# Modulation weights of a two-layer diffusion backbone loaded as 1 MB transfers instead of groups of four

## The chip, the cores and the metric

The kernel runs on one core of one Trainium2 chip. The metric is the device time of one execution in microseconds; several executions are made and their median is given. One further execution is taken with the hardware profiler, and all rows below come from it. Everything is computed in float32 accuracy.

## The reference, cut to what matters

Two layers of a diffusion backbone work on 1024 latent tokens and 256 context tokens of width 1024. Each layer starts from modulation vectors: a conditioning vector, one for the latent tokens and one for the context, times a weight matrix `w_mod` of 1024 rows by 6144 columns, plus `b_mod`:

```python
sh1, sc1, gt1, sh2, sc2, gt2 = jnp.split(mod_lat, 6, axis=-1)
h = rms_norm(x, g1) * (1 + sc1) + sh1
aq, ak, av, bq, bk, bv, cq, ck, cv, co, cg, dq, dk, dv = split_proj(h @ w_in)
...
x = x + gt1 * mix_out([ya, yb, yc, yd], g_group, w_out)
h2 = rms_norm(x, g2) * (1 + sc2) + sh2
x = x + gt2 * conv_ffn(h2, w_up, conv_w, conv_b, w_down)
```

So the first third of the modulation vector (`sh1`, `sc1`) is wanted before the input projection of its layer can begin; the other two thirds are wanted only behind attention. Four attention-like mixers (A to D) read slices of the one projection.

## The kernel before, in words

`w_mod` of a layer is cut into three sections of 2048 columns. `mod_section` computes one section: with the two conditioning vectors as the stationary operand (`self.stat[:, k]`, 128 rows by 32 columns, two of them used), it streams the weights through TensorE, for eight blocks of 128 rows (`k`). The 2048 columns are four groups `g` of 512; the product of group `g` goes to partitions 32g to 32g+31 of one PSUM tile (`modps`), that is to one of four column groups of the array. The finished sums are copied to SBUF (`modrow`), turned to features on partitions by four small products (`modo`) and added to the bias.

There are six sections, 48 MB of weights in all. The first (layer 0, section 0) runs in `start`, ahead of everything, with 512 columns in a piece: four transfers of 256 KB and four products 128x512 for each `k`, from a pool of 12 buffers. The other five run inside `phase1` of the two layers, as filler: `run` asks the generator `mods` for a step at every fourth step of the dense projections, which themselves are mixed with group A's attention. There the pieces have 256 columns: four transfers of 128 KB and four products 128x256 for each of 16 steps, from a pool of four buffers. Each step's transfers are written one step ahead of their products.

The order on each engine isn't written by hand. The program is given to a scheduler, which gives every instruction a priority by its place in the code and, by its own estimate of times, puts on each engine what it thinks can start next. The resulting order is fixed at build time; each engine then works through its list strictly in order and waits on semaphores. All transfers are issued by SyncE (SP), also in order: a transfer that has to wait for its buffer or its data holds up all that stand behind it. All of them go through one hardware queue.

Names in the rows: `wmod` the modulation weights, `stat` the stationary operand, `modps`, `modrow`, `modo` as above; `pj` the products of the input projection, `whi`/`wlo` and `hh`/`hl` the two parts of its weights and inputs; `xi`/`xt` the token-major inputs and their transposes; `ssq`, `ss`, `rsbc` the sums of the norm; `kt`/`kT` the keys of group A and their transposes; `S`, `mT`, `O`, `Y` group A's scores, maxima, values and outputs; `sX`, `sA_qk` scratch in HBM. One product of two float32 operands leaves two MATMUL records in the trace; a projection product, whose operands are the narrower parts, leaves one.

Of the kernel before, what the change touches and what calls it, by code (L numbers as in the profile page):

```python
# [29 lines left out]
# column chunks of the input projection: (name, ((first column, width) of each piece))  # L30
# [12 lines left out]
NB = (12, 4, 4)  # L43
# the mixer's second products: the order of the buffers of its inputs and of its weights
# [3 lines left out]
class Net:  # L48
# [40 lines left out]
    def weight(self, pool, src, eng, bufs, tag, raws=2, w=512, rawp=None):  # L89
        """The two parts of a weight block [P, 512] loaded from src, its first w columns used."""  # L90
# [15 lines left out]
    def mm3(self, out, terms, first=True, last=True, **kw):  # L106
        """out += sum of lhs.T @ rhs over terms ((lh, ll), (rh, rl)), float32 accuracy."""
# [46 lines left out]
    def cond_vector(self, st):  # L154
        """stat[:, k, 0:2] = silu of c and of c_ctx, features on partitions; the rest is zero."""
# [26 lines left out]
    def vectors(self, l, tile, t):  # L182
        nc, a = self.nc, self.a
        vp = self.vecp
        r1 = tile(name="r1")[0:112, 0:P]
        r2 = tile(name="r2")[0:88, 0:P]
# [10 lines left out]
        # the gated half of the conv carries the 1/2 of silu(x) = x (1 + tanh(x/2)) / 2  # L197
# [5 lines left out]
    def mod_section(self, l, sec, pool, pp, tag, modT, w=256):  # L203
        """modT[:, 16 sec + i, v]: features 128 i of section sec (2048 columns); v 0 latent, 1 context.
        Yields the time of each of its pieces."""
        nc, a = self.nc, self.a
        acc = pp.tile([P, 512], F32, tag=tag, name="modps")

        def load(n):
            W = []  # L210
            for g in range(4):
                W.append(pool.tile([P, w], F32, tag="raw", name="wmod"))
                c0 = sec * 2048 + g * 512 + n // KD * w
                nc.sync.dma_start(W[g], a["w_mod"][l, n % KD * P:(n % KD + 1) * P, c0:c0 + w])
# [12 lines left out]
        rows = [pool.tile([P, w], F32, tag="raw", name="modrow") for _ in range(512 // w)]  # L227
        for x, row in enumerate(rows):
            nc.scalar.copy(out=row, in_=acc[:, x * w:(x + 1) * w])
        yield 0.3  # L230
        o = pp.tile([P, 512], F32, tag=tag, name="modo")
        for b in range(4):
            nc.tensor.matmul(o[:, 8 * b:8 * b + 8], rows[b * P // w][:, b * P % w:b * P % w + P], self.sel8, start=True, stop=True)
# [7 lines left out]
    def rstd_rows(self, xs, n, p, pp, tag, most):  # L241
        """rs[:, i] = rstd of token 128 i + partition, for the n tokens of xs [P, KD, n]; most: the most tokens in p."""
# [23 lines left out]
    def rstd_cols(self, xs, n, p, pp, tag, most=256):  # L266
        """The rstd of the n tokens of xs [P, KD, n], on every partition."""
# [10 lines left out]
    def modulated(self, xs, bc, hi, lo, scale, bias, p=None):  # L278
        """hi + lo = xs * bc * scale + bias, in xs or by way of tiles of p; scale, bias [P, KD]."""
# [38 lines left out]
    def load_x(self, i, p, pp, tag):  # L318
        """Tile i of xT from the token-major inputs."""
# [15 lines left out]
    def phase1(self, l, modT, dst):  # L335
        """Norm 1, input projection, group A's attention, the preparation of groups C and D (its pools in dst)."""
        nc = self.nc
        with ExitStack() as st:
# [17 lines left out]
            mp = self.sb(st, f"wmods{l}", bufs=4)  # L356
            mps = self.ps(st, f"wmodp{l}")

            def modulation():
                yield from self.mod_section(l, 1, mp, mps, "mod", modT)  # L360
                if l == 0:
                    self.vectors(1, lambda name: mp.tile([P, 256], F32, tag="raw", name=name), mps.tile([P, 512], F32, tag="mod", name="vt"))
# [45 lines left out]
    def start(self, modT, wp, pm, ep):  # L408
        """The first layer's inputs: xT, the vectors, the modulation of norm 1, the weights of group A's columns."""
        with ExitStack() as s2:  # L410
# [6 lines left out]
            for _ in self.mod_section(0, 0, mp, pm, "mm", modT, 512):  # L417
                pass
            self.vectors(0, lambda name: ep.tile([P, 512], F32, tag="st", name=name), pm.tile([P, 512], F32, tag="mm", name="vt"))
# [5 lines left out]
    def norm1(self, l, modT, W, nrm, np_, pm, ep):  # L425
        """Norm 1, and the projection of group A's columns."""
# [44 lines left out]
    def proj_tiles(self, chunk, W, tiles, pm, ep):  # L471
        """A chunk's columns for the tiles, token-major."""
# [14 lines left out]
    def proj_cols(self, W, blocks, queries, out, pm, ep):  # L487
        """Column blocks of a chunk for all tokens, feature-major; the first ones are queries."""
# [11 lines left out]
    def rope(self, i, src, ep):  # L500
        """Rotates the heads src [P, 6, 64] of latent tile i - 2."""
# [65 lines left out]
    def out_d(self, f, p, x, ep):  # L567
        """Group D's query (the tokens of each tile in reverse) or key heads 2 f, 2 f + 1."""
# [30 lines left out]
    # Rows 0..9 are the forward chunks in scan order, rows 32..41 the backward ones; time runs forward in each row.  # L599
    def mlstm_steps(self, l, st):  # L600
        """Yields the time of its pieces, or of other work to put between them, and None once the gates are done."""
# [16 lines left out]
        with ExitStack() as s2:  # L618
# [41 lines left out]
            # running maximum across the chunks: m <- max(m, amax) + cend  # L660
# [63 lines left out]
        # ---- chunk sweeps  # L724
# [8 lines left out]
        at = [list(range(NT)), [1, 0] + list(range(NT - 1, 1, -1))]  # the tiles in scan order  # L733
# [102 lines left out]
    def group_norm(self, y, i, grp, p):  # L836
        """Stores y / rms(y) times the gain, over the 256 columns of one head group of tile i."""
# [44 lines left out]
    def prep_q(self, qt):  # L882
        """QH[:, h], QL[:, h]: the two parts of query head h, each on both halves of the partitions."""
# [871 lines left out]
```

## Time and profile before

| | us |
|---|---|
| median of 3 runs | 3538.09 (3537.04 to 3539.44) |
| the profiled execution's span, first to last instruction | 3548.8 |
| PE busy | 3416.7 (96%) |
| DVE busy | 2173.3 (61%) |
| ACT busy | 1497.2 (42%) |
| POOL busy | 955.8 (27%) |
| DMA, mean | 106 GB/s |

The profiled execution is 10.7 us longer than the median run. A row of the timeline gives the start in us from the span's start, the length, the engine, the source line, the operation, out<-in, the shape and the number of records that were merged, and in brackets the idle time ahead of it. Matmuls are pipelined, so lengths of neighbours overlap: what one costs is read from the distance of starts. In a shape as 128*32 128x256, 128*32 is the stationary operand and 256 the columns streamed.

### The profile page before, as it was taken

Reading aid. Unit: us, or ns where it says so; the run is one execution under the profiler, and the core shown is the slowest. Engines: PE = TensorE matmul, PEld = TensorE weight load, DVE = VectorE, ACT = ScalarE, POOL = GpSimd, SP = SyncE. Lnnn points to the kernel's source line nnn. Section 1 sums busy time; section 2 is a strip of 40 time slices with the busy share of each in tenths; the row PEclk is TensorE's granted clock in tenths of the full one; section 3 lists DMA queues with packets and bytes.
Section 4 is the critical chain, followed back from the end, with each engine's and each line's share of the span. In section 5 each row is a group of like instructions: output and inputs, shape, how many; then the busy total and the mean of one; then the engine's idle time right before and its main releaser. Section 6 shows DMA issues by size and latency. Waiting matters only on the chain. (4 is left out here: it accounts for less than half of the span.)

```text
span 3548.8 us, 53999 instructions
## 1 busy us (share of the span) xinstructions
PE 3416.7 (96%) x19949; PEld 2719.4 (77%) x19949; DVE 2173.3 (61%) x4103; ACT 1497.2 (42%) x3010; POOL 955.8 (27%) x1069
## 2 busy tenths in 40 slices
PE   8999999999997999999999999999999879999998
PEld 4776678776885888888888676877778758888887
DVE  4455452775438777778454745554774388888745
ACT  5334332556544444444120534423565454445311
POOL 2423233231344222220000623324222343332000
PEclk9999999999998999999999999999999989999999
DMA  8534344415331222215222534236233322222621
GB/s 285 156 104 124 96 115 125 126 51 159 117 107 54 64 72 64 74 63 204 85 83 78 144 109 121 68 105 170 64 121 96 99 63 86 75 90 75 219 83 60
DMA packets 437679, 377.61 MB, mean 106 GB/s; under 512 B 123048, under 2 KB 381224, under 8 KB 437416
## 3 DMA queue, kind: packets, MB, share of 16 engines
q1 hardware_dynamic: 437416, 374.17, 34.2%
q8 instruction: 157, 2.57, 0.3%
q14 instruction: 106, 0.87, 0.1%
HBM read 279.69 MB, written 94.37 MB: 105 GB/s over the span
## 5 line engine op out<-in xcount | busy, mean ns | idle before, releaser
L112 PE MATMUL b<-g,w 128*128 128x512 f32 (+1 forms) x880 | 321.9, 368 | 0.0
L113 PE MATMUL b<-g,w 128*128 128x512 f32 (+1 forms) x880 | 320.8, 368 | 0.0
L111 PE MATMUL b<-g,w 128*128 128x512 f32 (+1 forms) x880 | 320.1, 368 | 0.0
L1652 DVE SCALAR_TENSOR_TENSOR xT<-b,modT,xT 128x512 f32<-128x512 f32 (+1 forms) x280 | 191.5, 695 | 201.0 <-PE b L113 200.5
L111 PE MATMUL pj<-whi,hh 128*128 128x512 f32 (+2 forms) x800 | 282.8, 355 | 12.9 <-ACT v L554 5.4
L112 PE MATMUL pj<-wlo,hh 128*128 128x512 f32 (+2 forms) x800 | 281.4, 352 | 3.0 <-DVE wlo L103 3.0
L113 PE MATMUL pj<-whi,hl 128*128 128x512 f32 (+2 forms) x800 | 280.8, 352 | 0.0
L1526 POOL TENSOR_TENSOR s<-raw 128x512 f32<-128x512 f32 x88 | 118.2, 1343 | 471.0 <-DVE w L1533 381.5
L111 PEld LDWEIGHTS pj<-whi,hh 128*128 128x128 f32 x800 | 152.8, 191 | 49.8 <-issue 11.6
L112 PEld LDWEIGHTS b<-g,w 128*128 128x128 f32 x880 | 165.6, 189 | 27.5
L111 PEld LDWEIGHTS b<-g,w 128*128 128x128 f32 x880 | 165.5, 189 | 27.5
L113 PEld LDWEIGHTS b<-g,w 128*128 128x128 f32 x880 | 165.3, 188 | 27.7
L112 PEld LDWEIGHTS pj<-wlo,hh 128*128 128x128 f32 x800 | 153.0, 191 | 36.9 <-issue 15.0
L113 PEld LDWEIGHTS pj<-whi,hl 128*128 128x128 f32 x800 | 152.4, 191 | 35.5 <-issue 17.0
L1555 DVE SCALAR_TENSOR_TENSOR cg<-u,vec,cg 128x512 f32<-128x512 f32 (+1 forms) x176 | 166.4, 989 | 10.1 <-ACT cg L1550 10.1
L1532 ACT CAST w<-s 128x512 fp32r<-128x512 f32 x176 | 107.0, 618 | 155.1 <-PE b L113 103.5
L86 ACT CAST w<-raw 128x512 fp32r<-128x512 f32 x88 | 54.0, 620 | 271.1 <-PE b L113 241.7
L112 PE MATMUL o<-yl,wohi 128*128 128x256 f32 x576 | 164.9, 287 | 0.9 <-DVE yl L87 0.9
L113 PE MATMUL o<-yh,wolo 128*128 128x256 f32 x576 | 165.5, 288 | 0.1
L111 PE MATMUL o<-yh,wohi 128*128 128x256 f32 x576 | 164.9, 289 | 0.7 <-ACT yh L86 0.7
L1533 DVE TENSOR_TENSOR w<-raw,w 128x512 fp32r<-128x512 f32 x154 | 131.4, 867 | 54.0 <-ACT w L1532 53.9
L103 POOL TENSOR_TENSOR wolo<-raw,wohi 128x512 fp32r<-128x512 f32 x80 | 103.8, 1298 | 162.3 <-ACT wohi L102 148.0
(364 smaller groups left out, 9852.4 us busy)
## 6 DMA issues: line engine op xcount, KB each, us to landing
raw<-in_w_up_dram SPq DMA_DIRECT2D x176, 256.0 KB
wmod<-in_w_mod_dram SPq DMA_DIRECT2D x320, 128.0 KB
raw<-in_w_down_dram SPq DMA_DIRECT2D x88, 256.0 KB
raw<-in_w_in_dram SPq DMA_DIRECT2D x80, 256.0 KB
raw<-in_w_out_dram SPq DMA_DIRECT2D x80, 256.0 KB
sG<-cv SPq DMA_DIRECT2D x22, 640.0 KB
graw<-sG SPq DMA_DIRECT2D x22, 640.0 KB
sG<-cv SPq DMA_DIRECT2D x22, 512.0 KB
```

The costliest lines, as they stand in the source:

```text
L86: nc.scalar.copy(out=hi, in_=src)
L103: eng.tensor_tensor(lo[:, 0:w], raw[:, 0:w], f32v(hi[:, 0:w]), ALU.subtract)
L111: nc.tensor.matmul(out, lh, rh, start=(first and i == 0), stop=False, **kw)
L112: nc.tensor.matmul(out, lh, rl, start=False, stop=False, **kw)
L113: nc.tensor.matmul(out, ll, rh, start=False, stop=(last and i == n - 1), **kw)
L1526: nc.gpsimd.tensor_tensor(s, x, y, op)
L1532: nc.scalar.copy(out=hi, in_=src)
L1533: nc.vector.tensor_tensor(out=lo, in0=src, in1=f32v(hi), op=ALU.subtract)
L1555: nc.vector.scalar_tensor_tensor(out=o[:, x0:x1], in0=u[:, x0 - d - c:x1 - d - c], scalar=self.cw[w][:, j:j + 1], in1=o[:, x0:x1], op0=ALU ...
L1652: nc.vector.scalar_tensor_tensor(out=xs, in0=o[:, 0:t1 - t0], scalar=modT[:, 40 + f, v:v + 1], in1=xs, op0=ALU.mult, op1=ALU.add)
```

## The change

A section is loaded in eight transfers of 128 rows by 2048 columns (1 MB, 8 KB in a row) in place of 32 of 256 KB or 64 of 128 KB. Each lands in one tile that holds the four groups side by side, and the four products, now always 512 columns wide, read it. In `start` the pool has three such buffers (12 of 512 columns before, the same bytes); in `phase1` it has one (8 KB per partition; four of 1 KB before). As a step is now a whole block of 128 rows in both places, a section takes 8 steps and 2 for its end, where it took 16 and 2 in `phase1`. The staging buffer of `load_kv` for group A now comes from the tag of the maxima (`M`) in place of a pool of its own, and `vectors` gets one tile in place of two. What else is in the difference is comments that were dropped, which only moves line numbers (L223 becomes L214).

```diff
-NB = (12, 4, 4)
...
+NB = (3, 4, 4)
...
-    def mod_section(self, l, sec, pool, pp, tag, modT, w=256):
...
+    def mod_section(self, l, sec, pool, pp, tag, modT):
...
-        def load(n):
-            W = []
+        for k in range(KD):
+            W = pool.tile([P, 4, 512], F32, tag="raw", name="wmod")
+            nc.sync.dma_start(W.rearrange("p g f -> p (g f)"), a["w_mod"][l, k * P:(k + 1) * P, sec * 2048:(sec + 1) * 2048])
+            yield 0.5
             for g in range(4):
-                W.append(pool.tile([P, w], F32, tag="raw", name="wmod"))
-                c0 = sec * 2048 + g * 512 + n // KD * w
-                nc.sync.dma_start(W[g], a["w_mod"][l, n % KD * P:(n % KD + 1) * P, c0:c0 + w])
-            return W
-
-        W = load(0)
-        steps = 512 // w * KD
-        for n in range(steps):
-            yield 0.5
-            k, o = n % KD, n // KD * w
-            for g in range(4):
-                nc.tensor.matmul(acc[32 * g:32 * g + 32, o:o + w], self.stat[:, k, :], W[g],
+                nc.tensor.matmul(acc[32 * g:32 * g + 32], self.stat[:, k, :], W[:, g],
                                  start=(k == 0), stop=(k == KD - 1), skip_group_check=True)
-            if n < steps - 1:
-                W = load(n + 1)
...
-            mp = self.sb(st, f"wmods{l}", bufs=4)
+            mp = self.sb(st, f"wmods{l}")
...
-            for _ in self.mod_section(0, 0, mp, pm, "mm", modT, 512):
+            for _ in self.mod_section(0, 0, mp, pm, "mm", modT):
...
-                for _ in self.load_kv(KV, lambda: lp.tile([P, 512], F32, tag="kt", name="kt", bufs=2),
...
+            for _ in self.load_kv(KV, lambda: self.ap_.tile([P, 512], F32, tag="M", name="kt", bufs=2),
```

With other pieces the scheduler makes another order. Three places of it follow, the kernel before first.

TensorE in layer 0's phase 1, third section (`modps`), among projection products (`pj`), before:

```order
1653 L223 MATMUL modps<-wmod,stat 32x256
1654 L113 MATMUL pj<-hh_485,wlo 128x256
1655 L111 MATMUL pj<-hh_485,whi 128x256
1656 L223 MATMUL modps<-wmod,stat 32x256
1657 L112 MATMUL pj<-hl_486,whi 128x256
1658 L113 MATMUL pj<-hh_485,wlo 128x256
1659 L111 MATMUL pj<-hh_485,whi 128x256
1660 L223 MATMUL modps<-wmod,stat 32x256
1661 L112 MATMUL pj<-hl_486,whi 128x256
```

and now, in the same stage:

```order
1312 L1116 MATMUL S<-QL,ks 128x256
1313 L1115 MATMUL S<-QH,ks 128x256
1314 L1116 MATMUL S<-QL,ks 128x256
1315 L214 MATMUL modps<-wmod,stat 32x512 x4
1316 L111 MATMUL pj<-whi,hh_442 128x272
1317 L112 MATMUL pj<-wlo,hh_442 128x272
1318 L113 MATMUL pj<-whi,hl_443 128x272
```

Products that stood alone between others, each behind its own transfer, now stand as a run of four behind one transfer. Counted over the five sections of phase 1, the 320 products stood in 198 runs (136 of one product, 23 of two, 18 of three, 21 of four); the 160 products now stand in 51.

SyncE at the program's start, around the end of the first section's loads (`wmod`), before:

```order
16 L214 DMA wmod<-in_w_mod_dram 128x512 x4
17 L96 DMA raw<-in_w_in_dram 128x512 x2
18 L214 DMA wmod<-in_w_mod_dram 128x512 x4
19 L96 DMA raw<-in_w_in_dram 128x512 x2
20 L322 DMA xi<-in_x_dram 128x1024 x4
21 L452 DMA cos<-in_cos_dram 128x512
```

and now, with the last two loads of that section in row 31 (three stand in row 8, ahead of all others of this kind):

```order
22 L434 DMA sX<-xT 1024x1x256
23 L211 DMA wmod<-in_w_mod_dram 128x2048
24 L96 DMA raw<-in_w_in_dram 128x512 x4
25 L211 DMA wmod<-in_w_mod_dram 128x2048
26 L96 DMA raw<-in_w_in_dram 128x512 x4
27 L310 DMA xi<-in_x_dram 128x1024 x2
28 L434 DMA sX<-xT 1024x1x256
29 L310 DMA xi<-in_x_dram 128x1024 x2
30 L434 DMA sX<-xT 1024x1x256
31 L211 DMA wmod<-in_w_mod_dram 128x2048 x2
```

The section's last loads have moved behind all inputs `xi`, eight blocks of projection weights and three stores of `sX`.

TensorE at the end of that first section, before:

```order
18 L194 MATMUL vt<-ident,r_299 128x88
19 L327 MATMUL xt<-ident,xi 128x128 x16
20 L111 MATMUL pj<-whi,hh_483 128x512
21 L112 MATMUL pj<-wlo,hh_483 128x512
22 L111 MATMUL pj<-whi,hh_483 128x512
23 L112 MATMUL pj<-wlo,hh_483 128x512
24 L327 MATMUL xt<-ident,xi 128x128 x4
```

and now:

```order
29 L315 MATMUL xt<-ident,xi 128x128 x8
30 L247 MATMUL ss<-mean,nrow 128x1 x2
31 L241 MATMUL ssq<-nsq,ones 32x256 x8
32 L214 MATMUL modps<-wmod,stat 32x512 x4
33 L247 MATMUL ss<-mean,nrow 128x1 x2
34 L214 MATMUL modps<-wmod,stat 32x512 x4
35 L221 MATMUL modo<-sel_122,modrow 128x8 x4
36 L194 MATMUL vt<-ident,vr 128x112
37 L195 MATMUL vt<-ident,vr 128x88
38 L111 MATMUL pj<-whi,hh_434 128x512
```

All transposes of the inputs and all sums of the norm now stand ahead of the first projection product; before, 64 of the 80 transposes and 32 of the 40 `ssq` products stood behind it, mixed with the projection.

## Rows read from the trace of the kernel before

**Rows 1.** The page's head and its first part, TensorE and the others:
```profile
span 3548.8 us, 53999 instructions
PE 3416.7 (96%) x19949; PEld 2719.4 (77%) x19949; DVE 2173.3 (61%) x4103; ACT 1497.2 (42%) x3010; POOL 955.8 (27%) x1069
```
**Rows 2.** Busy time by stretch: stretch and its length, engines, clock, DMA share, GB/s:
```profile
core 0: us, PE busy (x) PEld busy (x) DVE busy (x) ACT busy (x) POOL busy (x), PEclk, DMA share, GB/s
0.00:106.00 106.00, 91.85 (x459) 57.14 (x460) 55.10 (x140) 50.79 (x115) 40.65 (x57) 1.00 0.74 249
...
400.00:501.00 101.00, 101.00 (x694) 74.02 (x693) 47.35 (x88) 34.52 (x70) 34.06 (x39) 1.00 0.31 94
...
2200.00:2300.00 100.00, 100.00 (x727) 77.81 (x726) 55.51 (x102) 45.12 (x94) 34.40 (x31) 1.00 0.25 79
```
**Rows 3.** Groups by line, 106 to 501 and 1998 to 2251 us, modulation products:
```profile
L223 PE MATMUL modps<-wmod,stat 128*32 128x256 f32 x384 | 79.1, 391 | 0.1
...
L223 PE MATMUL modps<-wmod,stat 128*32 128x256 f32 x256 | 45.1, 391 | 0.0
```
**Rows 4.** Timeline of TensorE: one product alone (two records) among others:
```profile
435.33 0.28 PE L1130 MATMUL S<-QL,ks 128*128 128x256 f32 x1
435.54 0.62 PE L223 MATMUL modps<-wmod,stat 128*32 128x256 f32 x2
436.09 0.38 PE L112 MATMUL pj<-wlo,hh 128*128 128x256 f32 x1
436.31 0.28 PE L113 MATMUL pj<-whi,hl 128*128 128x256 f32 x1
```
**Rows 5.** Timeline of TensorE: four products in a run (eight records):
```profile
457.00 0.28 PE L1130 MATMUL S<-QL,ks 128*128 128x256 f32 x1
457.21 0.64 PE L223 MATMUL modps<-wmod,stat 128*32 128x256 f32 x8
457.78 0.38 PE L112 MATMUL pj<-wlo,hh 128*128 128x256 f32 x1
458.00 0.28 PE L113 MATMUL pj<-whi,hl 128*128 128x256 f32 x1
458.12 0.28 PE L111 MATMUL pj<-whi,hh 128*128 128x256 f32 x1
```
**Rows 6.** Timeline of TensorE: three products of 512 columns in a run:
```profile
18.18 1.06 PE L223 MATMUL modps<-wmod,stat 128*32 128x512 f32 x6
```
**Rows 7.** Timeline of TensorE: first and last run of phase 1's products:
```profile
107.71 0.64 PE L223 MATMUL modps<-wmod,stat 128*32 128x256 f32 x8
...
2237.91 0.62 PE L223 MATMUL modps<-wmod,stat 128*32 128x256 f32 x2
```
**Rows 8.** Timeline of TensorE: end of the first section, first projection product:
```profile
32.83 3.04 PE L223 MATMUL modps<-wmod,stat 128*32 128x512 f32 x8 [1.74 <-DMA wmod<-in_w_mod_dram]
36.55 1.06 PE L233 MATMUL modo<-sel,modrow 128*128 128x8 f32 x8 [0.68 <-ACT modrow L229]
...
40.90 0.50 PE L111 MATMUL pj<-whi,hh 128*128 128x512 f32 x1
```
**Rows 9.** Busy time by stretch, the first 60 us:
```profile
0.00:60.00 60.00, 47.48 (x235) 23.10 (x236) 20.77 (x58) 24.82 (x51) 5.59 (x11) 1.00 0.97 345
```
**Rows 10.** Groups by line on TensorE, 38 to 110 us:
```profile
L327 PE MATMUL xt<-ident,xi 128*128 128x128 f32 x63 | 8.9, 277 | 1.7 <-DVE xT L333 1.7
L253 PE MATMUL ssq<-nsq,ones 128*32 128x256 f32 x64 | 7.3, 391 | 0.1
```
**Rows 11.** Timeline of SyncE: two issues held up or merged in layer 0 and 1:
```profile
86.72 5.83 SPq L541 DMA_DIRECT2D sA_v<-v  x2
...
2002.14 1.80 SPq L214 DMA_DIRECT2D wmod<-in_w_mod_dram  x4
```
**Rows 12.** Timeline of TensorE: the products behind that load of layer 1:
```profile
2005.99 0.39 PE L113 MATMUL pj<-whi,hl 128*128 128x512 f32 x1
2006.22 0.49 PE L870 MATMUL kT<-ident,kt 128*128 128x128 f32 x3
2006.64 1.44 PE L223 MATMUL modps<-wmod,stat 128*32 128x256 f32 x8
```
**Rows 13.** The line of the products, 110 to 2260 us, waits for loads:
```profile
  DMA wmod<-in_w_mod_dram: 0.9, 4
```

More of the change, by code (lines that the diff above doesn't have):

```diff
@@ L179, in cond_vector, with vectors @@
             in1=h.rearrange("p (v k) -> p v k", v=2), op0=ALU.add, op1=ALU.mult)
-    def vectors(self, l, tile, t):
+    def vectors(self, l, r, t):
         nc, a = self.nc, self.a
         vp = self.vecp
-        r1 = tile(name="r1")[0:112, 0:P]
-        r2 = tile(name="r2")[0:88, 0:P]
+        r1 = r[0:112, 0:P]
+        r2 = r[0:88, P:2 * P]
         cw = a["conv_w"]
@@ L200, in vectors @@
         self.vecs[l] = dict(g1=v[:, 0:8], g2=v[:, 8:16], cw=[v[:, 24:68], v[:, 68:112], v[:, 112:156]], cb=v[:, 156:200])
-    def mod_section(self, l, sec, pool, pp, tag, modT, w=256):
+    def mod_section(self, l, sec, pool, pp, tag, modT):
         nc, a = self.nc, self.a
         acc = pp.tile([P, 512], F32, tag=tag, name="modps")
-        def load(n):
-            W = []
+        for k in range(KD):
+            W = pool.tile([P, 4, 512], F32, tag="raw", name="wmod")
+            nc.sync.dma_start(W.rearrange("p g f -> p (g f)"), a["w_mod"][l, k * P:(k + 1) * P, sec * 2048:(sec + 1) * 2048])
+            yield 0.5
             for g in range(4):
-                W.append(pool.tile([P, w], F32, tag="raw", name="wmod"))
-                c0 = sec * 2048 + g * 512 + n // KD * w
-                nc.sync.dma_start(W[g], a["w_mod"][l, n % KD * P:(n % KD + 1) * P, c0:c0 + w])
-            return W
-        W = load(0)
-        steps = 512 // w * KD
-        for n in range(steps):
-            yield 0.5
-            k, o = n % KD, n // KD * w
-            for g in range(4):
-                nc.tensor.matmul(acc[32 * g:32 * g + 32, o:o + w], self.stat[:, k, :], W[g],
-                                 start=(k == 0), stop=(k == KD - 1), skip_group_check=True)
-            if n < steps - 1:
-                W = load(n + 1)
-        rows = [pool.tile([P, w], F32, tag="raw", name="modrow") for _ in range(512 // w)]
-        for x, row in enumerate(rows):
-            nc.scalar.copy(out=row, in_=acc[:, x * w:(x + 1) * w])
+                nc.tensor.matmul(acc[32 * g:32 * g + 32], self.stat[:, k, :], W[:, g],
+                                 start=(k == 0), stop=(k == KD - 1), skip_group_check=True)
+        row = pool.tile([P, 4, 512], F32, tag="raw", name="modrow")[:, 0]
+        nc.scalar.copy(out=row, in_=acc)
         yield 0.3
@@ L232, in mod_section @@
         for b in range(4):
-            nc.tensor.matmul(o[:, 8 * b:8 * b + 8], rows[b * P // w][:, b * P % w:b * P % w + P], self.sel8, start=True, stop=True)
+            nc.tensor.matmul(o[:, 8 * b:8 * b + 8], row[:, b * P:b * P + P], self.sel8, start=True, stop=True)
         bm = self.bm[l][:, sec * 16:(sec + 1) * 16].rearrange("p (g b) -> p b g", b=4)
@@ L361, in modulation @@
                 if l == 0:
-                    self.vectors(1, lambda name: mp.tile([P, 256], F32, tag="raw", name=name), mps.tile([P, 512], F32, tag="mod", name="vt"))
+                    self.vectors(1, mp.tile([P, 4, 512], F32, tag="raw", name="vr")[:, 0, 0:256], mps.tile([P, 512], F32, tag="mod", name="vt"))
                     yield
@@ L416, in start @@
                 self.load_x(i, xp, lp, "lx")
[L417 removed]
+            for _ in self.mod_section(0, 0, mp, pm, "mm", modT):
                 pass
[L419 removed]
+            self.vectors(0, ep.tile([P, 512], F32, tag="st", name="vr"), pm.tile([P, 512], F32, tag="mm", name="vt"))
             W = self.proj_weights(0, C_A, wp, rp, NB[2])
@@ L1043, in attn_a @@
             self.use(pools)
-            with ExitStack() as s2:
-                lp = self.sb(s2, f"ald{l}", side=side)
-                KV = self.open_kv(kp, 2)
-                for _ in self.load_kv(KV, lambda: lp.tile([P, 512], F32, tag="kt", name="kt", bufs=2),
-                                      self.sA_qk, self.sA_v, 2, 4, self.asp):
-                    pass
+            KV = self.open_kv(kp, 2)
+            for _ in self.load_kv(KV, lambda: self.ap_.tile([P, 512], F32, tag="M", name="kt", bufs=2),
+                                  self.sA_qk, self.sA_v, 2, 4, self.asp):
+                pass
             jobs, fetch = self.jobs_ab(0, pools, *KV, self.sA_qk, None, None)
```

## The prediction

> **What bounds the kernel now.** I read the page's head first. TensorE is busy for 3416.7 of 3548.8 us [rows 1], but 96% over a whole program says nothing of one stage, so I asked for the busy time by stretch next. The change touches two stretches of each layer: the start, and phase 1, where modulation products are filler between projection products and attention. In phase 1 TensorE is busy for all 101.0 of 101 us in layer 0 and all 100.0 of 100 us in layer 1, while DVE stands at about half, ACT at 35 to 45%, POOL at a third, DMA at 25 to 31% [rows 2]. There the only thing that ends later is TensorE's own list: a microsecond taken from it should be a microsecond of the program. The first 60 us are different: the DMA engines are 0.97 busy at 345 GB/s [rows 9] and TensorE waits for modulation weights [rows 8]. There bytes decide, and the order in which SyncE asks for them.
>
> Then I looked at what one modulation product costs in TensorE's timeline. The group view gives 79.1 us and 45.1 us for 640 records, 124.2 us in all [rows 3], but lengths of pipelined matmuls overlap, so I read distances of starts. A product alone: from the score matmul ahead of it (435.33) to the second matmul behind it (436.31) are 0.98 us [rows 4]. Without it these two steps would take 2 x 0.12 us, the distance of neighbours of 256 columns [rows 5]. It adds 0.74 us. Four products in a run: 457.00 to 458.00, 1.00 us, so 0.76 us for all four [rows 5]. The four column groups run at the same time; what costs is the run, not the product: the change to 32-column operands and back, and one stream.
>
> **The change part by part.**
>
> *Fewer runs.* From the first run of phase 1 to the last [rows 7] there are 198 runs before, by count of the order, and 51 now. Before: 198 x 0.75 = 148.5 us. (The group view agrees: 124.2 / 198 = 0.63 us, to which the slower first step behind a run comes.) Now a run streams 512 columns. No such run stands in phase 1 before; in the start three products of 512 columns took 1.06 us [rows 6] against 0.64 us for four of 256 [rows 5], 0.42 us more. So 51 x (0.75 + 0.42) = 59.7 us. Saved on TensorE: 89 us. Bounds: this is the most it can save; if products of 512 columns did not overlap at all, each product behind the first of its run would add twice that 0.42 us, 109 x 0.84 = 92 us, and nothing would be saved. I take the near end, since rows 6 show three overlapping.
>
> The Trainium skill (TensorE: Matmul & The Clock Gate, Part 3 on packing small matmuls) gives measured speedups short of the number of tiles: 2.38 for three column groups, 3.07 for four row groups. By that four would take 1.3 times as long as one, some 0.26 us more for each run, 13 us in all, and the sum would be 13 us higher. The trace speaks against it: 0.62 us for one product, 0.64 for four [rows 4, 5].
>
> *The start.* Before, the first section's products end at 35.87 and the first projection product begins at 40.90, 5.0 us later [rows 8]. Now the last two loads of the section stand behind, by SyncE's order: 1 MB of context, three and then three more loads of 1 MB, eight blocks of projection weights (2 MB), all of x (4 MB), cos and sin (0.5 MB) and three stores of sX (3 MB); with these two 19.5 MB of 2^20 bytes, 20.4e6 bytes. The chip moved 60 us x 345 GB/s = 20.7e6 bytes in its first 60 us [rows 9]. So these land at about 60 us, their products end near 61, and the projection begins near 66, 25 us later than before. Against that stands work that TensorE now does while it waits, and did behind that point before: the transposes (8.9 us) and the norm's sums (7.3 us) [rows 10], 16 us. Net loss 9 us; I take 10, with 0 (all hidden) and 25 (nothing regained) as bounds. The bytes themselves are the same.
>
> *One buffer, loads four times as large.* A load in phase 1 can only be issued when the run before it has ended, and SyncE issues in order. Before, this cost almost nothing: four waits, 0.9 us [rows 13]. How long does 1 MB take? No row shows a load of that size with 8 KB rows. The tightest row is in layer 1: four loads of 128 KB, 1.80 us to issue them from 2002.14 [rows 11]; the products behind took 1.44 us in place of 0.64 [rows 12], so the last could begin at about 2007.4, 5.3 us from the first issue. One load of 1 MB saves three issues (some 1.4 us) and adds 0.52e6 bytes at 345 GB/s [rows 9], 1.5 us: 5.4 us. Between two loads' runs stand 39 to 87 other matmuls (median 53; one gap of 24) in the order. At 0.12 to 0.23 us each [rows 5, 12], and with a change of operand size or two, that is 6.5 to 8.5 us, an estimate. So the load is covered but in the one short gap. I take 5 us in all; bounds 0, and 30 us for the rival below.
>
> *The rest.* 160 instead of 320 products, and five copies in place of ten to `modrow` on ACT, lie on an engine at 35 to 45% [rows 2]: nothing; if that cover were gone, five copies are 2 us. The key staging that now shares the buffers of the maxima M waits for nobody, since no maximum is due before the keys are in; if one were, it would be once a layer, a microsecond. Transfers fall from 352 to 48; SyncE, though in order, was not late [rows 13]. Bytes and all later stages stay, and the order of the channel mixer is the same; I give 0, with 5 us either way.
>
> **Sum.** -89 + 10 + 5 = -74 us against the profiled execution: 3548.8 - 74 = 3474.8. That execution stands 10.7 us above the median run, so 3464 us is what I forecast for the median.
>
> **The rivals.**
>
> *The loads are late by a little everywhere.* If a load takes 8.2 us from the end of a run to the next, TensorE waits about 0.7 us at each of the 40 loads of phase 1 beyond 7.5 us of cover: 28 us in place of 5, so 3487 us. For it: other traffic of 79 to 94 GB/s goes through the same queue [rows 2], and there is one buffer. Against it: the 5.4 us above. The Trainium skill (DMA: Bandwidth & Descriptors, Bandwidth) has 6.15 us for a transfer of 1 MB, to which its fixed cost of about 2 us comes: that is where 8.2 comes from; its figures are for transfers that GpSimd issues, these are SyncE's.
>
> *SyncE holds the loads up; slower.* An issue stands behind a store that waits for its data: before, two stores to `sA_v` occupied the queue for 5.83 us [rows 11]. If every 1 MB load stood behind one such, it would land after 5.4 + 5.8 = 11.2 us, TensorE would wait 3.7 us at each of 40, 148 us in place of 5: 3607 us. It decides from a wait of 2.0 us a load (79 / 40), a load of 9.5 us. Against it: four times as many issues stood in the same queue before and cost 0.9 us [rows 13].
>
> *The change doesn't do what it says: wide products don't overlap.* Then 92 us come on top, 3556 us. Rows 6 speak against it.
>
> *The start costs nothing.* Everything that waits is filled with moved work, no load is late: 3464 - 15 = 3449 us.
>
> **How the numbers follow.** The forecast 65%, the late loads 15%, the free start 13%, SyncE's hold-up 4%, no overlap 3%. The range from 3440 to 3506: below, the free start and the 5 us of the rest and some; above, the late loads and 25 us of the start's bound. It leaves out the last two rivals and some of each end. A measurement of this kernel tells 0.2% (7 us) from no change. Faster by more: the first three, 93%. Within 0.2%: 2%, slower: 5%, from the last two.
>
> **What would show it.** Right: in the timeline of phase 1 runs of eight records of 512 columns some 1.06 us long; TensorE still at 100% there, the stretch from 106 us on shorter by 40 to 45 us in layer 0 and about 30 us in layer 1, the stages behind unchanged; the first projection product near 66 us. Wrong: a wait for `wmod` of a microsecond or more ahead of most runs (late loads), SyncE's own waits ahead of `wmod` (hold-up), runs of 2 us or more (no overlap). If another engine comes near 100% in phase 1, or the projection begins after 75 us, my sum is wrong at its first or second term.

## The result and the profile after

| | before | after |
|---|---|---|
| median, us | 3537.57 (3531.82 to 3539.44) | 3475.53 (3473.32 to 3480.21) |
| ratio to before | | 0.9829, 95% interval [0.9817, 0.9841] |
| span of the profiled execution, us | 3548.8 | 3471.6 |

The change gains 62 us. I had forecast 74 us, so the direction and the largest term were right and the amount was 12 us too large.

The first two lines of the page, of the changed kernel and then of a second profile of the kernel before (they answer to [rows 1]):

```profile
span 3471.6 us, 52832 instructions
...
PE 3332.2 (96%) x19629; PEld 2698.5 (78%) x19629; DVE 2178.5 (63%) x4103; ACT 1498.5 (43%) x3005; POOL 967.1 (28%) x1069
```

```profile
span 3533.6 us, 53999 instructions
...
PE 3412.6 (97%) x19949; PEld 2718.2 (77%) x19949; DVE 2174.7 (62%) x4103; ACT 1499.1 (42%) x3010; POOL 956.3 (27%) x1069
```

Span less PE's busy time is TensorE's idle time: 121.0 us before, 139.4 us after. So TensorE has 80.4 us less to do and idles 18.4 us more; the difference of the two is the 62 us. What follows is about these two numbers.

The first starts of certain tiles on TensorE cut the program into stages (`kT` is the first key transpose, `gt` the first transpose of the gates, `b` the first product of the channel mixer):

| stage, us | before, first profile | before, second | after |
|---|---|---|---|
| begin to kT, layer 0 | 106.0 | 104.7 | 110.4 |
| kT to gt, layer 0 (phase 1) | 394.7 | 394.8 | 356.1 |
| gt to b, layer 0 | 554.7 | 547.6 | 547.9 |
| b to first projection of layer 1 | 899.7 | 898.2 | 900.7 |
| to gt, layer 1 (phase 1) | 396.2 | 395.2 | 372.0 |
| gt to b, layer 1 | 476.8 | 472.1 | 463.2 |
| b to the end | 720.5 | 720.8 | 721.3 |

Against the second profile, 61.9 us go in the two phases 1, 8.9 us behind that of layer 1, and 5.7 us are lost at the start. TensorE's 18.4 us of further idle time lie mostly at the start too: ahead of the first key transpose it idles 28.4 us, 13.6 before.

The groups of the modulation products in the stretches 106 to 470 and 1960 to 2290 us of the changed kernel (line engine operation, shape, count | busy, mean ns | idle before, releaser) answer to [rows 3]:

```profile
L214 PE MATMUL modps<-wmod,stat 128*32 128x512 f32 x184 | 33.9, 605 | 1.7 <-DMA wmod<-in_w_mod_dram 1.7
...
L214 PE MATMUL modps<-wmod,stat 128*32 128x512 f32 x128 | 19.1, 605 | 3.1 <-DMA wmod<-in_w_mod_dram 3.1
```

124.2 us have become 53.0 us (for 156 of the 160 products; one run stands ahead of 106 us), and TensorE waited 4.8 us for weights. One run of four in the timeline of the changed kernel (start, length, then as before) answers to [rows 5]:

```profile
204.01 0.28 PE L111 MATMUL pj<-hh,whi 128*128 128x256 f32 x1
204.22 1.07 PE L214 MATMUL modps<-wmod,stat 128*32 128x512 f32 x8
205.21 0.39 PE L112 MATMUL pj<-hl,whi 128*128 128x256 f32 x1
205.44 0.28 PE L113 MATMUL pj<-hh,wlo 128*128 128x256 f32 x1
```

From 204.01 to 205.44 are 1.43 us; without the run these two steps take 2 x 0.12, so it adds 1.19 us (forecast 1.17). Measured so for every run behind the first key transpose (start of the row ahead to start of the second row behind, less the median of the same neighbours without a run), 198 runs add 150.4 us before (first profile; about 152 in the second), median 0.75, and 50 runs add 67.7 us after, median 1.18. That is 82.7 us for the 80.4 by which PE's busy time fell.

The start, answering to [rows 8], with two loads that came late:

```profile
36.81 1.06 PE L214 MATMUL modps<-wmod,stat 128*32 128x512 f32 x8 [0.62 <-DMA wmod<-in_w_mod_dram]
42.03 1.94 PE L214 MATMUL modps<-wmod,stat 128*32 128x512 f32 x8 [4.16 <-DMA wmod<-in_w_mod_dram]
...
63.11 1.06 PE L221 MATMUL modo<-sel,modrow 128*128 128x8 f32 x8 [0.71 <-ACT modrow L217]
66.44 0.79 PE L111 MATMUL pj<-whi,hh 128*128 128x512 f32 x1 [2.04 <-ACT hh L277]
```

The first projection product begins at 66.44 us, 40.90 before. And the busy time by stretch (stretch and length, PE, PEld, DVE, ACT, POOL, granted clock, DMA share, GB/s), answering to [rows 2, 9]:

```profile
0.00:60.00 60.00, 37.65 (x237) 21.36 (x239) 15.92 (x40) 24.49 (x44) 3.47 (x8) 0.80 0.95 358
...
300.00:400.00 100.00, 98.30 (x745) 76.83 (x744) 54.70 (x105) 48.12 (x101) 39.41 (x35) 1.00 0.33 114
2100.00:2200.00 100.00, 98.31 (x761) 82.35 (x761) 65.12 (x126) 50.94 (x107) 41.52 (x37) 1.00 0.26 82
```

Phase 1 is still TensorE's, but with a few more gaps: 98.3 in place of 100 in these stretches, and 15.9 us of idle time between the first key transposes and the gates of both layers, 10.9 in the first profile of before. The first 60 us have a granted clock of 0.80 in place of 1.00 (0.86 in the second profile of the changed kernel).

### The profile page after: what moved, and what is told of

Read it like the earlier page. It is cut to its first block, busy times and chain, and to the rows that moved or that the text cites. A ratio compares the mean times of both kernels' runs of the same rounds, so it can differ in the third digit from the quotient of the medians.

```text
span 3471.6 us, 52832 instructions
## 1 busy us (share of the span) xinstructions
PE 3332.2 (96%) x19629; PEld 2698.5 (78%) x19629; DVE 2178.5 (63%) x4103; ACT 1498.5 (43%) x3005; POOL 967.1 (28%) x1069
```

## The experiments

My theory: what is paid in phase 1 is the run (the change to 32-column operands and back, and one stream), whatever the number of products in it; the change pays because the one transfer makes the four products possible at once, so that the scheduler puts them together. Rivals: the size of the transfers, or the width and number of the products, is the gain. Beside it: what the start costs, and whether a microsecond off TensorE is one off the program.

All in one table first. Runs and what they add are those behind the first key transpose; idle is span less PE busy; "told fours" means that the order is told to keep the four products of a step together; ratios are to the kernel before on the same chip. The chips differ: the median of the kernel before was 3542.0 us beside "changed, told fours", "the same, start in order" and "old start, no products", and 3537.6 to 3538.9 beside the others, so kernels of different chips are better compared by their ratios than by their medians.

| kernel | runs | add | PE busy | idle | median | ratio [95%] |
|---|---|---|---|---|---|---|
| before, second profile (add: first) | 198 | 150.4 | 3412.6 | 121.0 | 3538 | |
| changed, second profile | 50 | 67.5 | 3330.9 | 140.1 | 3477.3 | 0.9829 [0.9815, 0.9842] |
| old start | 54 | 69.9 | 3336.1 | 133.3 | 3475.5 | 0.9827 [0.9809, 0.9845] |
| new start only | 190 | 152.1 | 3408.1 | 151.2 | 3558.6 | 1.0056 [1.0043, 1.0070] |
| one 512 KB load, 256 wide | 97 | 81.0 | 3352.9 | 126.5 | 3480.8 | 0.9836 [0.9823, 0.9849] |
| four loads, 512 wide | 127 | 153.6 | 3419.7 | 125.5 | 3547.9 | 1.0028 [1.0017, 1.0040] |
| old start, told fours | 39 | 55.2 | 3331.6 | 137.1 | 3466.6 | 0.9800 [0.9786, 0.9813] |
| before, told fours | 80 | 64.5 | 3337.1 | 137.9 | 3476.2 | 0.9820 [0.9806, 0.9833] |
| changed, told fours | 39 | 51.7 | 3321.0 | 150.5 | 3474.1 | 0.9805 [0.9790, 0.9820] |
| the same, start in order | 39 | 55.4 | 3323.9 | 144.7 | 3470.2 | 0.9801 [0.9786, 0.9816] |
| old start, no products | 4 | 6.7 | 3291.7 | 137.1 | 3429.7 | 0.9679 [0.9664, 0.9694] |
| four loads, told fours | 39 | 48.7 | 3324.9 | 129.7 | 3456.8 | 0.9772 [0.9757, 0.9786] |

**The old start with the new phase 1.**

```diff
-NB = (3, 4, 4)
+NB = (12, 4, 4)
...
-            for _ in self.mod_section(0, 0, mp, pm, "mm", modT):
+            for _ in self.mod_pieces(0, 0, mp, pm, "mm", modT, 512):   # mod_section of the kernel before
```

> Phase 1 as changed (1 MB transfers, one buffer, products of 512 columns one behind the other); the start as before (32 transfers of 256 KB, 12 buffers of 512 columns). By its order 54 runs of modulation products behind the first key transpose, 50 in the changed kernel. Theory (the start of the changed kernel costs about 15 us, because the first projection waits for the last two 1 MB loads): first projection product back near 41 us, granted clock of the first 60 us back to 1.00 from 0.80; 15 us gained, 4 more runs at 1.17 us lost: 3475.5 - 15 + 5 = 3465 us. Rival (the start only moves work about and costs nothing): 3475.5 + 5 = 3480 us.

3475.5 us: the theory's 3465 failed as a total. Half of it holds by stage: first projection at 39.7 us, clock 1.00 in the first 60 us, and layer 0 up to `b` takes 999.4 us against 1014.4 in the changed kernel, 15.0 us less. Layer 1 gave 12.8 us of it back (from `b` on 2470.0 us against 2457.2): 23 runs there for 18, and waits in attention. No line of layer 1's code differs between the two; its order does.

**The new start with the old phase 1.**

```diff
-NB = (12, 4, 4)
+NB = (3, 4, 4)
...
-            for _ in self.mod_section(0, 0, mp, pm, "mm", modT, 512):
+            for _ in self.mod_whole(0, 0, mp, pm, "mm", modT):   # mod_section of the changed kernel
```

> The start as changed (eight transfers of 1 MB, three buffers); phase 1 as before (transfers of 128 KB, products of 256 columns). 190 runs in phase 1, 198 before. Theory (start costs 15 us, a run 0.75 us): 3537.6 + 15 - 8 x 0.75 = 3547 us, first projection near 66 us. Rival (start is free): 3537.6 - 6 = 3532 us. If my forecast's 10 us hold: 3542 us.

3558.6 us, 20 us slower than before: a start that costs, and more than either number of mine. First projection at 65.6 us; layer 0 up to `b` takes 1071.7 us for 1047.2 in the second profile of before. By these two comparisons the start costs 15 to 25 us in layer 0; with the other profile of the changed kernel (1012.7) and of the kernel before (1055.4) they give 13 and 16.

**One transfer, but 256 columns.**

```diff
-            W = pool.tile([P, 4, 512], F32, tag="raw", name="wmod")
+            W = pool.tile([P, 4, 256], F32, tag="raw", name="wmod")
-            nc.sync.dma_start(W.rearrange("p g f -> p (g f)"), ...)
+            nc.sync.dma_start(W, src[k * P:(k + 1) * P, :, o:o + 256])   # 512 KB, four pieces per row
```

> The start as before. In phase 1 one transfer of 512 KB per step, 128 rows by four pieces of 256 columns, into one tile (two buffers, together the 8 KB of the changed kernel's one); the products stay 256 columns wide and there are 320 of them, as before, but the four of a step become possible at once: 97 runs by its order, 198 before. Theory (what is paid is the run, 0.75 us at 256 columns): 97 x 0.75 = 73 us in place of 148.5: 3537.6 - 76 = 3462 us. Rival (what is gained lies in half as many, wider products or in 1 MB transfers): same number and width of products, so no change: 3537 us.

3480.8 us. The same 320 products of 256 columns as before, in half as many runs, bring 58 us: neither the width nor the number of products is the gain. Of 69.4 us less in runs, 58 arrive.

**Four transfers, but 512 columns.**

```diff
-            nc.sync.dma_start(W.rearrange("p g f -> p (g f)"), a["w_mod"][l, k * P:(k + 1) * P, sec * 2048:(sec + 1) * 2048])
+            for g in range(4):
+                nc.sync.dma_start(W[:, g], a["w_mod"][l, k * P:(k + 1) * P, sec * 2048 + g * 512:sec * 2048 + g * 512 + 512])
```

> The start as before. In phase 1 the one tile of 8 KB and the products of 512 columns as in the changed kernel, but the tile is filled by four transfers of 256 KB, one for each product: 127 runs by its order, 111 of them a single product. Theory (the run is paid, 1.06 to 1.17 us at 512 columns whether one product or four): 135 to 149 us in place of 148.5 before: 3524 to 3538 us, nearly all of the gain gone. Rival (wider products and fewer steps make the gain, the size of a transfer does not matter): as the changed kernel with the start before, 3460 to 3465 us.

3547.9 us, 9 us slower than before: the whole gain is gone with the same tile, the same products and the same order of loops. The timeline of this kernel shows why:

```profile
307.15 0.28 PE L112 MATMUL pj<-wlo,hh 128*128 128x272 f32 x1
307.37 1.04 PE L215 MATMUL modps<-wmod,stat 128*32 128x512 f32 x2
308.35 0.39 PE L113 MATMUL pj<-whi,hl 128*128 128x272 f32 x1
308.57 0.29 PE L111 MATMUL pj<-whi,hh 128*128 128x272 f32 x1
308.70 0.29 PE L112 MATMUL pj<-wlo,hh 128*128 128x272 f32 x1
308.83 0.29 PE L113 MATMUL pj<-whi,hl 128*128 128x272 f32 x1
309.05 1.05 PE L215 MATMUL modps<-wmod,stat 128*32 128x512 f32 x2
```

One product (two records) lasts 1.04 us, four (eight records) 1.07; from 307.15 to 308.57 are 1.42 us, against 1.43 for four above. The groups of the two phases read

```profile
L215 PE MATMUL modps<-wmod,stat 128*32 128x512 f32 x192 | 84.6, 609 | 0.2 <-DMA wmod<-in_w_mod_dram 0.2
...
L215 PE MATMUL modps<-wmod,stat 128*32 128x512 f32 x128 | 51.3, 605 | 0.0
```

135.9 us for 160 products, where 156 take 53.0 us in the changed kernel. The Trainium skill (TensorE: Matmul & The Clock Gate, Part 3 on packing small matmuls) has speedups short of the number of tiles, 3.07 for four row groups; by that four would last 1.3 times one, an estimate. Here four last 1.07 us and one 1.04, so that four column groups gain a factor of 3.9.

**The kernel before, once more.**

```diff
 (no line differs)
```

> The kernel before once more, nothing changed, for a second profile of it. The first profile's span was 3548.8 us, 10.7 us above the median of the runs, and my forecast took these 10.7 us off the changed kernel as well. Theory (the first profile caught a long execution, and the excess lies in stages that the change does not touch): a span near 3537 us, the stretch from the first key transpose to the first product of the mixer's gate within 3 us of 394.7 and 353.2 us again, and the stages behind shorter by about 10 us in sum. Rival (a profiled execution of this kernel is always some 10 us longer than an unprofiled one): about 3549 us again, the same stages as in the first profile.

3533.6 us span. Of the 15.2 us that the first profile was longer, 7.1 lie from `gt` to `b` in layer 0 and 4.7 in layer 1, and 0.9 in the two phases 1 (table of stages). So the 77 us between the two first profiles overstate the gain; the medians' 62 us are right, and to subtract the 10.7 us was, too.

**The changed kernel, once more.** (No line differs.)

> The changed kernel once more, nothing changed, beside the same runs of the kernel before as the other kernels of this group. Theory (median to median is the right comparison): ratio 0.982 to 0.984, 3475 us, profile within 5 us of it. Rival (the 77 us between the two profiles are the real difference): 3461 us.

0.9829 again, span 3471.0 us: it repeats.

**Fours told to the order.** `issue_after` queues what follows behind an instruction of the same engine, `high_priority` takes it as soon as it can start.

```diff
+            first = product(0)
+            with self.tc.issue_after(first), self.tc.high_priority():
+                for g in range(1, 4):
+                    product(g)
```

> As the kernel with 1 MB transfers in phase 1 and the start as before (3475.5 us), but the order is told to put products two to four of a block right behind the first: 39 runs of four behind the first key transpose, where that kernel had 54 runs of one to four (69.9 us added in its trace) for the same 156 products, bytes, transfers and buffer. Theory (the run is paid, 1.18 us each): 39 x 1.18 = 46 us, 24 us less: 3452 us, with 10 us either way for what a new order does to the attention stages behind. Rival (short runs cost in proportion to their products, the sum is fixed): 3475 us, no change.

3466.6 us, 10.7 less than the changed kernel in the same group; 9 less than with the old start, of 24 expected. The runs add 55.2 us where I had 46: 3.6 of these 9 are waits for weights, the rest I can't tell apart. Of the 14.7 us that runs are cheaper, 9 arrive.

**Only the order.** The kernel before, its transfers, buffers, width and start untouched:

```diff
+            last = product(3)
+            with self.tc.issue_after(last), self.tc.high_priority():
+                for g in range(3):
+                    product(g)
```

> The kernel before with its transfers of 128 KB, four buffers, products of 256 columns and start all untouched; only the order in phase 1 is told to put the other three products of a step right behind the one whose weights are loaded last: 80 runs of four, 198 runs before. Theory (the run is paid, 0.75 us each, and the change's 1 MB transfers matter only because they make the four products possible at once): 80 x 0.75 = 60 us in place of 149: 89 us gained, 3538 - 89 = 3449 us, with 10 us either way for the order behind. Rival (the large transfers or the half as many steps are worth something by themselves): slower than the changed kernel's 3475 us; if nothing but these counted, 3538 us.

3476.2 us: four lines that move no byte otherwise give all that the change gives. So 1 MB is not needed for it. Of 85.9 us less in runs 62 arrive; 89 were expected. Its groups:

```profile
L223 PE MATMUL modps<-wmod,stat 128*32 128x256 f32 x384 | 30.7, 391 | 1.1 <-DMA wmod<-in_w_mod_dram 1.0
...
L223 PE MATMUL modps<-wmod,stat 128*32 128x256 f32 x256 | 20.9, 399 | 0.6 <-DMA wmod<-in_w_mod_dram 0.6
```

51.6 us for the 640 records that took 124.2 [rows 3].

**Fours in the changed kernel.** The edit of the fours above, on the changed kernel.

> The changed kernel, its start included, with products two to four of each block told to follow the first directly: 39 runs behind the first key transpose (50 in the changed kernel, which added 67.5 us in its second trace). Theory A (terms add up from the changed kernel: 39 x 1.18 us and 8 us of waits, 54 us): 3477 - 13 = 3464 us. Theory B (terms add up from the kernel with the old start and runs of four, 3466.6 us, plus a start of 14 us): 3480 us. What lies between says how far terms add up at all. Rival for the run price: no change, 3477 us, with A and B not to be told apart from it unless the runs in the trace cost other than 1.18 us each.

3474.1 us, between the two. The runs add 51.7 us, as theory A has it, and PE is busy 9.9 us less than in the changed kernel; it idles 10.4 us more, so the profile is as long (3471.5 us for 3471.0). But this chip is the slower one: by the ratios, 0.9805 for 0.9829, some 8 of the 16 us by which the runs are cheaper arrive, with intervals that overlap. Against the old start with the same 39 runs, layer 0 up to `b` takes 1006.7 us for 998.8: a third comparison of the starts, 8 us apart, and here the ratios differ by 0.0005.

**The start's transfers in another order.** To the same kernel:

```diff
-            W = self.proj_weights(0, C_A, wp, rp, NB[2])
-            for i in range(2, NT):
-                self.load_x(i, xp, lp, "lx")
+            with self.tc.issue_after(self.last_load):
+                W = self.proj_weights(0, C_A, wp, rp, NB[2])
+                for i in range(2, NT):
+                    self.load_x(i, xp, lp, "lx")
```

> As the kernel with the changed start and runs of four, with the same eight 1 MB transfers and three buffers in the start; only SyncE's order is told: projection weights but four, and the tokens of x, are asked for behind the section's last load. Ahead of that load then stand some 10.5 MB instead of 19.5. Theory (the start is late by what stands ahead in the queue, not by the size of a transfer or the three buffers): the section ends near 37 us as in the kernel before, first projection product at 42 to 47 us, granted clock of the first 60 us back towards 1.00, 10 to 15 us faster than with the changed order. Rival (1 MB transfers in three buffers are late by themselves, each waits for a whole block's products): first projection product at 55 us or later, under 5 us gained.

3470.2 us, 4 less, inside the intervals. The first projection moved from 65.9 to 48.5 us, so what stands ahead in the queue does set it; but the time did not follow. Stretch and TensorE's waits up to 112 us (engine, what waited, for what: us, times, longest) in this kernel:

```profile
0.00:60.00 60.00, 35.67 (x191) 20.04 (x192) 17.22 (x47) 18.32 (x38) 4.09 (x9) 0.80 0.84 320
```

```profile
PE modps L215 <- DMA wmod<-in_w_mod_dram: 15.3, 8, 7.6
PE rsbc L269 <- DVE ndg L268: 4.5, 2, 2.6
```

and in the changed kernel:

```profile
PE modps L214 <- DMA wmod<-in_w_mod_dram: 7.3, 5, 4.2
PE xt L315 <- DMA xi<-in_x_dram: 4.6, 2, 2.6
```

Told to keep the order, SyncE takes 11.68 us to issue four loads, of which it waits 4.0 us for products that still read a buffer and 5.9 us for earlier loads to land:

```profile
22.35 11.68 SPq L211 DMA_DIRECT2D wmod<-in_w_mod_dram  x4
```

DMA falls from 354 GB/s in the same kernel without the told order to 320 GB/s, TensorE waits 15.3 us in place of 7.3 + 4.6, and the clock is no better, 0.80 (0.86 without the told order). Ahead of the first key transpose TensorE idles 29 us in either order. That the three buffers are the reason is not shown.

**What a microsecond off TensorE is worth.** To the old start with fours:

```diff
-            first = product(0)
+            if k == 0:   # and the other three; blocks 1 to 7 are not multiplied
+                first = product(0)
```

> As the kernel with the old start and runs of four (3466.6 us), but of the eight blocks of a section in phase 1 only the first is multiplied: the products of the seven others are left out, all transfers and the rest stay. 5 runs of 40 remain, 6 us of 55 added. It measures what a microsecond taken off TensorE in phase 1 is worth. Rival (one for one, as my forecast took it): 3466.6 - 49 = 3418 us, and the time up to the first product of layer 0's second mixer product less what the runs add stays at 960 to 969 us. Theory (a fifth to a quarter comes back as waits behind phase 1, as the kernels so far have it: 950 us there with 97 us of runs, 961 with 38, 969 with 30): some 38 us, 3428 us, and 973 to 980 us there.

3429.7 us (theory 3428, rival 3418), and 979.2 us up to `b` less what runs add (981.6 - 2.4). 48.5 us less in runs bring 36.9 between the medians. But the two kernels ran on different chips; by the ratios, 0.9679 for 0.9800, they bring 43 us, which lies between theory and rival. In the profiles PE is busy 39.9 us less and the span is 39.9 us shorter: idle time is 137.1 us in both. So over the whole program no idle time came back here; in phase 1 of layer 0 it rose from 5.9 to 14.1 us, and behind it fell as much. The phase 1 of layer 0 without the products, and what TensorE waited for there:

```profile
119.00:458.00 339.00, 324.90 (x2363) 279.79 (x2361) 178.28 (x342) 140.00 (x292) 117.53 (x119) 0.96 0.42 136
```

```profile
PE pj L111 <- ACT v L571: 6.1, 2, 4.3
PE S L1158 <- DVE M L1162: 3.7, 1, 3.7
PE modo L227 <- ACT modrow L223: 2.1, 1, 2.1
```

The waits are for ACT's and DVE's small results (`v`, `M`), and the granted clock is 0.96 there, 0.99 with all products (119 to 450 us) and 1.00 before [rows 2].

**Four loads, fours told.** The loads of the experiment with four transfers, the order of the fours:

```diff
+            last = product(3)
+            with self.tc.issue_after(last), self.tc.high_priority():
+                for g in range(3):
+                    product(g)
```

> As the kernel with four transfers of 256 KB for each block in phase 1 (one tile, products of 512 columns, the old start; 127 runs behind the first key transpose, 3547.9 us): the same transfers, tile and products, only the order is told to put the first three products of a block right behind that of the last transfer: 39 runs of four. Theory (the one transfer of 1 MB matters because it makes four products possible at once; told the order, four transfers do as well): runs add 50 to 56 us in place of 154, of these 100 us some 80 reach the end: 3466 us as with 1 MB transfers and runs of four, 10 us either way. Rival (1 MB transfers are worth something by themselves, or four issues in the queue cost): 3480 us or more. Rival (terms go one for one): 3448 us.

3456.8 us, 91 us less than the same transfers and products without the told order, and the fastest: 0.9772 [0.9757, 0.9786], clear of the changed kernel's 0.9829 [0.9815, 0.9842]. Page and groups:

```profile
span 3454.6 us, 53001 instructions
...
PE 3324.9 (96%) x19629; PEld 2694.9 (78%) x19629; DVE 2177.7 (63%) x4103; ACT 1497.3 (43%) x3005; POOL 961.6 (28%) x1069
```

```profile
L215 PE MATMUL modps<-wmod,stat 128*32 128x512 f32 x192 | 25.6, 606 | 0.8 <-DMA wmod<-in_w_mod_dram 0.8
...
L215 PE MATMUL modps<-wmod,stat 128*32 128x512 f32 x128 | 17.1, 605 | 1.0 <-DMA wmod<-in_w_mod_dram 1.0
```

Its idle time is 129.7 us, 7.4 less than with 1 MB transfers and the same runs. From issue to landing (KB each, median us) a load takes, here and in the changed kernel:

```profile
wmod<-in_w_mod_dram SPq DMA_DIRECT2D x192, 256.0 KB, 4.3
```

```profile
wmod<-in_w_mod_dram SPq DMA_DIRECT2D x48, 1024.0 KB, 6.5
```

The Trainium skill (DMA: Bandwidth & Descriptors, Bandwidth) has the rule to batch transfers to 1 MiB or more. It speaks for the change; these runs do not: with the same runs of products, 256 KB gave a ratio of 0.9772 and 1 MB 0.9800 [0.9786, 0.9813], not clearly apart, with 256 KB on the better side.

## Why the prediction was right, and where its size was off

- *Phase 1 is bound by TensorE, and the run is paid, not the product: right.* One product and four take the same (1.42 and 1.43 us at 512 columns), and the kernels with 39 to 198 runs follow what their runs add, that is their number at 0.75 us (256 columns) or 1.18 us (512), whatever the size of the transfers: 127 runs of 512 columns add 153.6 us and leave the kernel about as slow as 198 of 256 columns, with 150.4.
- *Fewer runs, -89 us: -82.7 measured.* The price was right (1.17, measured 1.18; 0.75 as said). 50 runs add 67.7 us, not 59.7; of the 8 us between, 4.8 are waits for loads, which I had as a term of their own, 5 us. Together -84 forecast, -82.7 found: this step stands. Its sign in the stages, 40 to 45 us in layer 0 and about 30 in layer 1, came out as 38.7 and 23.2 us, both below.
- *Four column groups overlap at 512 columns, no 92 us on top: right.*
- *The start, +10 us (0 to 25): the place was right, the size stays open.* The first projection was forecast at 66 us and found at 66.44. The list of bytes in front of the last loads adds up to 18.5 MB, not 19.5; in the trace of the changed kernel SyncE issues twelve blocks of projection weights there, not eight, so the total holds. Of the 64 transposes counted as moved work, 16 stood ahead of the projection before as well, so that some 14 us were moved and not 16. The three comparisons have layer 0 longer by 8, 13 to 15, and 16 to 25 us, so 10 is at the low end of them. I counted the work that TensorE can do meanwhile at full clock; it idled, and the granted clock fell to 0.80 in that stretch. By the totals the start can't be priced: the old start in the changed kernel ends at the same 3475.5 us, and the new start in the kernel before costs 20.
- *"A microsecond taken from it should be a microsecond of the program": too much for what the runs add; how far it fails is not settled.* Against the kernel before, of 80.5 us less in runs 63 arrive with the old start, of 95.2 us 72 with fours, of 85.9 us 62 with the order alone, of 101.7 us 82 in the fastest; with one 512 KB load, 58 of 69.4. That is 72 to 84%. Idle time is higher in all five (121.0 us before, 126.5 to 137.9 in them), part of it in phase 1, part in the attention behind, and the mean granted clock is a little lower (0.977 to 0.981 for 0.982); these carry part of the rest. Taking the products away is the cleanest test and speaks less clearly: 36.9 of 48.5 us by the medians, 43 by the ratios, and no more idle time in all. In the changed kernel itself the loss lies in layer 0, with the start: in layer 1 its runs add 26 us less than in the second profile of before, and the way from the first projection to `b` is 32 us shorter. At 100% of TensorE in [rows 2] the others looked free at 35 to 55%, but the waits of layer 0 in the experiment without products are for short results of theirs; that TensorE's own length had hidden these before is my reading of it, not shown by a run.
- *The rest, 0 with 5 us either way: too narrow.* A new order alone moves the stretch from `gt` to `b` by more: in layer 1 it took 463.2 us in the changed kernel, 468.5 with the old start, 488.0 with the order alone (some jobs can cross the boundary).
- *10.7 us from profile to median: right*, as the second profile shows.
- *The rivals.* Late loads everywhere: no, 4.8 us in 50 runs. SyncE's hold-up: no. The 8.2 us, an estimate that I added up from two figures of the Trainium skill (DMA: Bandwidth & Descriptors; 6.15 us in Bandwidth, about 2 us in Anatomy of one DMA), stood against medians of 5.3 to 6.5 us in the profiles here. A free start: not in layer 0.

So the runs are -82.7 and the result is -62. The start takes 8 to 25 of the 21 us between, and what the rest is, and its sign, no row settles.

What stays open: how much of the start is the order of its transfers and how much the three buffers (the order alone did not cure it; more buffers were not tried), and why the attention stages move by up to 20 us with the order.

## What to carry to other kernels

Count how often TensorE changes its kind of operand, not its small products: products for different column groups cost one when they follow each other, and each when they stand alone. With a scheduler, check in the order that what belongs together stands together; telling it so gave here as much as a new layout of the transfers, and 82 us with the better of both. And when the binding engine is relieved, do not count on all of it: against the kernel before, 72 to 84% of what the runs no longer added reached the end here.

## What the runs showed of the hardware

A gap in TensorE's work cost more than its length. In the changed kernel it waited 4.16 us ahead of the run at 42.03; that run then took 1.94 us in place of 1.06, the first projection product 0.79 us in place of 0.50 [rows 8]. In stretches of 10 us of the changed kernel:

```profile
10.00:20.00 10.00, 5.49 (x49) 2.05 (x48) 2.76 (x7) 5.34 (x10) 1.19 (x1) 1.00 0.92 345
...
40.00:50.00 10.00, 5.80 (x24) 3.31 (x24) 4.08 (x6) 3.25 (x6) 0.00 (x0) 0.50 1.04 397
...
80.00:95.00 15.00, 14.14 (x60) 10.85 (x60) 14.63 (x39) 11.44 (x29) 8.03 (x10) 1.00 0.26 66
```

A granted clock of 0.50 is the lower of the two levels, 1.2 of 2.4 GHz, for the whole stretch; it was 1.00 again from 80 to 95 us. Over the whole program the mean clock is 0.982 in the kernel before and 0.976 in the changed one (0.978 in its second profile). By the medians, a transfer of 256 KB landed after 4.3 us in the fastest kernel and one of 1 MB after 6.5 us in the changed one (5.8 in its second profile, 5.3 with the old start), so four times the bytes took between a quarter and a half longer.
